# A two-layer decoder in split fp32: the first layer's operand sums, the B sums of its first chunk, the sweep's weights and the modulation's columns are placed anew

## The chip, the core and the metric

The kernel runs on one NeuronCore of a Trainium2 chip. The core has a matrix engine (TensorE, PE in the profile; PEld is its loading of weights), VectorE (DVE), ScalarE (ACT), GpSimd (POOL) and SyncE (SP), which work through queues of their own, each in order, and wait for one another by semaphores. Sixteen DMA engines move data between the chip's memory and the core's. The metric is the device time of one execution in microseconds (us); lower is better. The time before is the median of three runs.

## What is computed

A sequence of 512 tokens of width 1024 goes through two layers; each is a mixer and an MLP, both modulated by a vector `c`:

```python
def modulate(h, shift, scale):
    return h * (1.0 + scale[:, None, :]) + shift[:, None, :]
...
ada = silu(c) @ ada_w + ada_b        # six vectors a layer: shift, scale, gain, twice
h = modulate(rmsnorm(x, g), shift, scale)
x = x + gain * mixer(h)              # layer 0: pooling, layer 1: spatial gating (SGU)
h = modulate(rmsnorm(x, g), shift, scale)
x = x + gain * (square(relu(h @ w1)) @ w2)   # width 1024 -> 4096 -> 1024
```

This is a condensed form of the reference. All of it is float32. In the SGU, `z = gelu(h @ w_in)` is split into u and v, v is normed and mixed along the tokens by `w_s`, and `(u * mixed) @ w_out` is the mixer's output.

## The kernel before

**Products in three parts.** Each float32 operand is split into a high and a low part of the type that TensorE takes. For weights, `split` has ScalarE write `wh` (line 176) and VectorE write `wl` (line 177); for activations `parts` does the same (lines 620 and 621, `oh`/`ol`, `hb`, `as`). `mm3` makes one product of three matmuls: `wl` by high (line 186), `wh` by low (187), `wh` by high (189); in the second product of an MLP the activations are the stationary side and the names stand the other way round. A weight thus passes DMA, ScalarE and VectorE before TensorE can use it, and both engines take such steps strictly in their order.

**The MLP in units.** Both matrix products are cut into blocks and partly done by Strassen and Winograd's scheme of seven products. `mlp` runs a list of `units` in a fixed order on TensorE:

- f(c,f): column tile f of column chunk c of the first product, plain: 48 matmuls of 256 columns.
- s(c,j,m): product m of Strassen's seven for half j of chunk c of the first product: 24 matmuls of 256 columns.
- p(c,m): product m of the seven of the second product over chunk c: 24 matmuls of 512 columns.
- q(dh,t): the last plain part of the second product.

The seven come in the order 1, 5, 6, 3, 7, 2, 4. In layer 0 a sweep of seven column tiles over all of the depth comes first (`sweep_load`, `sweep_hi`, `sweep_lo`; weights `wk`, seven times 128 columns wide), then unit 0 is f(0,7), units 1 to 3 are f(1,0) to f(1,2), and 4 to 15 are p(0,1), f(1,3), p(0,5), f(1,4), p(0,6), f(1,5), p(0,3), f(1,6), p(0,7), f(1,7), p(0,2), p(0,4). Units 16 to 18 are s(2,0,1), s(2,0,5), s(2,0,6), 19 is p(1,1), 20 and 21 are s(2,0,3) and s(2,0,7), 22 is p(1,5); more s and p follow, and 58 to 65 are the q. In layer 1 all column chunks but the first use s units: 0 to 3 are f, 4 to 66 are three rounds of s and p, 67 to 74 the q.

**B sums.** The seven products need sums of w2's blocks. `b_of` loads a block (tile `bt`, one buffer, for the chain; tile `b` otherwise), and `b_add` adds the next block to a tile with an accumulating DMA on GpSimd's queue (line 833). In each chunk `bt` passes m = 1, 5, 6, 4 that way: after each use the next block is added. A fourth accumulating transfer adds block 22 to block 12 for m = 7. The flag `by_dma` is constant here.

**A sums.** In layer 0, `a_parts` (steps at units `A_PARTS`) makes the sums of h's blocks that the s units read (`as`, lines 701, 702, 713, 620, 621). Its scratch is the pool `su`, whose tiles `s` and `u` the p units use too.

**Modulation's columns.** 56 tiles of `ada_w` (tile `ada`, 128x1024, 512 KB each) are loaded by SP's queue (line 205) and reduced by one VectorE operation each (line 209), two of them making a pair of `mods` (line 194). `ex` tells at which unit a tile is issued. In layer 0, `COLUMNS` gives 24 tiles their units; tiles 12 to 18 use the buffer `gb` (one), the others the pool `w4` (three), which the raw weights use too. In the SGU 19 tiles are issued in the u phase, three a step, and five in the output projection (w_o), one a step. In layer 1 eight tiles go to `gb`, at units 8, 10, ... 22. `spread_cols` turns eight `mods` columns into a row by a transpose on TensorE and two DMAs; the row is the MLP's gain.

**What sets the order.** TensorE's order is that of the code. On the other engines a scheduler places each instruction at build time and moves those up that can run, so an operation issued at unit n can stand well ahead of that unit's work. An operation that waits there holds up everything behind it on its engine.

Of the kernel before, what the change touches and what calls it, by code (L numbers as in the profile page):

```python
# [45 lines left out]
def c_g(n, k):  # L46
    return 24 * n + 16 + k
# [29 lines left out]
COLUMNS = (0, 1, 2, 3, 4, 5, 6, 7, 8, 9, 10, 11, 18, 23, 28, 33, 38, 43, 48, 58, 59, 60, 61, 61)  # L77
A_PARTS = (12, 13, 14, 16)
# [3 lines left out]
def decoder_kernel(ctx: ExitStack, tc: tile.TileContext, xtok, vecs, rows, fgrow, ada0, adag, ada1, pool_w, w1s, w1, w1f, w1b, w2, w2e, w_v, w_u, w_o, wsT, lnp, bs, out):  # L82
# [119 lines left out]
    def ada_tile(i, t, src, get):  # L202

        r = get()
        nc.sync.dma_start(r, src)
        b, j = divmod(t, 2)
        if j == 0:
            pmv[i, b] = sm.tile([P, 2], F32, name="pmv", tag="pmv")
        V.scalar_tensor_tensor(r, r, 1.0, cb, ALU.mult, ALU.mult, accum_out=pmv[i, b][:, j : j + 1])  # L209
        if j == 1:  # L210
            finish_mods(i, b, pmv.pop((i, b)))
# [46 lines left out]
    with (  # L258
# [367 lines left out]
    def mlp(i, first, extra, last, ending):  # L626
# [3 lines left out]
        with (  # L630
# [56 lines left out]
            def a_parts(step):  # L687

                blocks = [[H(slice(4 * j, 4 * j + 4), slice(256 * r, 256 * r + 256)) for j in range(2)] for r in range(2)]

                def operand(pool, tag):
                    o = pool.tile([P, 2, 4, 256], F32R, name="as", tag=tag)
                    return o[:, 0], o[:, 1]

                def scratch(tag):
                    return su.tile([P, 4, 256], F32, name="a" + tag, tag=tag)

                def difference(p, q):
                    t, u = scratch("s"), scratch("u")
                    for n, o in enumerate((t, u)):  # L700
                        V.tensor_tensor(o, f32(p[n]), f32(q[n]), ALU.subtract)
                    V.tensor_tensor(t, t, u, ALU.add)
# [120 lines left out]
            by_dma = True  # L823
            held = {}

            def b_of(c, r, n, chain=False):
                kw = dict(name="bt", tag="bt", bufs=1) if by_dma and chain else dict(name="b", tag="b", bufs=3 - by_dma)
# [7 lines left out]
            def p_prep(u):  # L835
# [9 lines left out]
                elif m == 5:  # L845
                    wb = B["t"]
                    if not by_dma:
# [4 lines left out]
                elif m == 6:  # L852
                    wb = B["t"]
                    if not by_dma:
# [6 lines left out]
                elif m == 3:  # L861
                    if by_dma:
                        wb = b_of(c, 1, 1)
                        B["b12"] = b_of(c, 0, 1)
                    else:
                        wb = B["b22"]
                    a = B.pop("s")
                    V.tensor_tensor(a, quad(c, 0, 1), a, ALU.add)
                elif m == 7:
                    wb = B.pop("b12")  # L870
                    if not by_dma:
                        V.tensor_tensor(wb, wb, B.pop("b22"), ALU.add)
                    a = B.pop("u")
                elif m == 2:
                    wb = B["b21"] = b_of(c, 1, 0)
                    a = quad(c, 0, 1)
                else:
                    wb, b21 = B.pop("t"), B.pop("b21")
                    if not by_dma:
                        V.tensor_tensor(wb, wb, b21, ALU.add)  # L880
# [5 lines left out]
                if by_dma:  # L886

                    nxt = {1: 5, 5: 6, 6: 4}.get(m)
                    if nxt:
                        b_add(wb, c, *CHAIN[nxt])  # L890
                    if m == 3:
                        b_add(B["b12"], c, 1, 1)
# [43 lines left out]
            def q_prep(u):  # L936
# [8 lines left out]
                else:  # L945
                    o = w2p.tile([P, 2, KD, P], F32R, name="qo", tag="b", bufs=3 - by_dma)
# [135 lines left out]

    def modulation(q, get):

        return lambda: ada_tile(0 if q < 8 else 1, 40 + q if q < 8 else q - 8, ada1[q], get)
# [17 lines left out]
    with (  # L1103
# [42 lines left out]
        ex += [modulation(q, get4) for q in range(32, 43)]  # L1146
# [33 lines left out]
        ex += [modulation(q, get4) for q in range(43, 48)]  # L1180
        h_[0] = hparts(GAP)
        h32.append(ytile("h32").rearrange("p t d -> p (t d)").rearrange("p (k s) -> p k s", k=KD))
        for dh in range(2):
# [4 lines left out]
            for t, ks in ((0, range(early)), (1, range(early)), (0, range(early, KD)), (1, range(early, KD)), (2, range(KD)), (3, range(KD))):  # L1188
# [57 lines left out]
    ex = [(8 + 2 * q, modulation(48 + q, late_gb if q == 0 else get_gb)) for q in range(8)]  # L1246
    ex += [(30, lambda: spread_cols(mods[1][:, c_g(1, 0) : c_g(1, 0) + KD], "gain1"))]
# [81 lines left out]
```

## Time and profile before

| | us |
|---|---|
| median of 3 runs | 899.78 (895.88 to 901.6) |
| the profiled execution | 898.25 |
| its span in the profile | 896.5 |
| TensorE busy | 857.0 (96%) |
| VectorE busy | 685.5 (76%) |
| ScalarE busy | 467.8 (52%) |
| mean granted clock of TensorE | 0.989 |

The profile is of one execution. A row of the timeline gives start, duration, engine, line and operation, and in brackets how long the engine stood idle before it and what ended that idle time. Matmuls overlap: each is shown some 0.28 or 0.39 us long, while the next starts earlier. The granted clock of TensorE is 1.00 over most of the span and 0.50 in a few spells of 3.4 or 6.8 us. The views by stretch of time give the busy time of each engine within it, so that a stage can be read apart from the mean.

### The profile page before, as it was taken

To read this page: it belongs to the slowest core of one execution; us is meant where nothing else is said; L and a number is where in the kernel's file an instruction comes from. 1 tells how busy PE (TensorE), PEld (TensorE's weight loads), DVE (VectorE), ACT (ScalarE), POOL (GpSimd) and SP (SyncE) were. 2 spreads that over 40 slices of the span, in tenths; PEclk is the share of its full clock that TensorE was granted. 3 is DMA by queue.
4 is the path that set the end of the run, shared out by engine and by line. 5 is a ranking of instruction groups with operands and counts; after the bars stand their busy time and mean duration, and the time that the engine had idled before them with its cause. 6 is when DMAs were issued, how large, how long until landed. Compare 5 with 4: busy or idle time off the path is not lost. (4 is left out here: it accounts for less than half of the span.)

```text
span 896.5 us, 13013 instructions
## 1 busy us (share of the span) xinstructions
PE 857.0 (96%) x5116; PEld 758.1 (85%) x5116; DVE 685.5 (76%) x918; ACT 467.8 (52%) x682; POOL 66.7 (7%) x91
## 2 busy tenths in 40 slices
PE   8999998897999999999999999999897999999996
PEld 7778997786899989888888778999896999989885
DVE  6889466897898688677798856666788698779855
ACT  5285636344576377347332325665755476547521
POOL 3000000001001010000010001000001110110001
PEclk9999999998999999999999999999999999999999
DMA  8968986768587866535748613946787877767402
GB/s 353 417 242 309 347 247 188 227 225 218 125 228 196 202 143 236 212 118 211 245 155 267 210 57 147 323 101 168 190 280 192 204 182 241 165 146 249 145 24 94
DMA packets 43507, 184.43 MB, mean 206 GB/s; under 512 B 4892, under 2 KB 5044, under 8 KB 36151
## 3 DMA queue, kind: packets, MB, share of 16 engines
q1 hardware_dynamic: 35282, 137.72, 41.9%
q0 software_dynamic: 7728, 43.53, 23.9%
q10 hardware_dynamic: 436, 2.37, 0.8%
q8 instruction: 40, 0.66, 0.3%
q14 instruction: 21, 0.16, 0.1%
HBM read 177.29 MB, written 6.30 MB: 205 GB/s over the span
## 5 line engine op out<-in xcount | busy, mean ns | idle before, releaser
L186 PE MATMUL po<-hb,wl 128*128 128x256 f32 (+1 forms) x696 | 207.3, 298 | 3.7 <-DVE wl L177 3.2
L187 PE MATMUL po<-hb,wh 128*128 128x256 f32 (+1 forms) x696 | 206.1, 296 | 0.2 <-DVE hb L621 0.2
L189 PE MATMUL po<-hb,wh 128*128 128x256 f32 (+1 forms) x697 | 205.9, 296 | 0.0
L177 DVE TENSOR_TENSOR wl<-raw,wh 128x1024 fp32r<-128x1024 f32 (+1 forms) x122 | 145.4, 1195 | 32.7 <-ACT wh L176 32.5
L176 ACT ACTIVATE wh<-raw 128x1024 fp32r<-128x1024 f32 (+1 forms) x122 | 125.5, 1034 | 76.9 <-DVE raw L774 22.5
L186 PEld LDWEIGHTS po<-hb,wl 128*128 128x128 f32 x696 | 131.4, 189 | 9.4 <-DVE wl L177 3.1
L187 PE MATMUL pm<-wl,oh 128*128 128x512 f32 x336 | 131.5, 391 | 5.0 <-DVE wl L177 5.0
L187 PEld LDWEIGHTS po<-hb,wh 128*128 128x128 f32 x696 | 132.0, 190 | 4.6 <-DVE hb L621 0.4
L189 PEld LDWEIGHTS po<-hb,wh 128*128 128x128 f32 x697 | 131.9, 189 | 4.3
L186 PE MATMUL pm<-wh,ol 128*128 128x512 f32 x336 | 131.4, 391 | 1.3 <-DVE ol L621 1.2
L189 PE MATMUL pm<-wh,oh 128*128 128x512 f32 (+1 forms) x375 | 131.2, 367 | 0.0
L209 DVE SCALAR_TENSOR_TENSOR ada<-ada,cb 128x1024 f32<-128x1024 f32 x56 | 68.3, 1221 | 53.7 <-DMA ada<-in_ada 53.4
L177 DVE TENSOR_TENSOR wl<-bt,wh 128x1024 fp32r<-128x1024 f32 x48 | 57.8, 1222 | 45.0 <-ACT wh L176 45.0
L189 PEld LDWEIGHTS pm<-wh,oh 128*128 128x128 f32 x375 | 70.5, 188 | 14.8
L186 PE MATMUL po<-as,wl 128*128 128x256 f32 x240 | 69.1, 288 | 13.6 <-ACT g L810 8.2
L176 ACT ACTIVATE wh<-bt 128x1024 fp32r<-128x1024 f32 x48 | 49.5, 1052 | 61.0 <-DMA bt<-in_w 54.7
L187 PEld LDWEIGHTS pm<-wl,oh 128*128 128x128 f32 x336 | 63.2, 188 | 17.7 <-DVE wl L177 6.1
L186 PEld LDWEIGHTS pm<-wh,ol 128*128 128x128 f32 x336 | 63.2, 188 | 13.8 <-DVE ol L621 1.9
L189 PE MATMUL po<-as,wh 128*128 128x256 f32 x240 | 68.3, 285 | 0.0
L187 PE MATMUL po<-as,wh 128*128 128x256 f32 x240 | 68.3, 285 | 0.0
L186 PEld LDWEIGHTS po<-as,wl 128*128 128x128 f32 x240 | 47.0, 196 | 14.9 <-ACT g L810 8.6
L1037 ACT ACTIVATE tmp<-x 128x512 f32<-128x512 f32 (+1 forms) x25 | 15.3, 612 | 66.8 <-DVE x L1033 53.0
(216 smaller groups left out, 1555.4 us busy)
## 6 DMA issues: line engine op xcount, KB each, us to landing
ada<-in_ada SPq DMA_DIRECT2D x72, 512.0 KB, 4.6
raw<-in_w1b SPq DMA_DIRECT2D x40, 512.0 KB, 5.6
b<-in_w SPq DMA_DIRECT2D x18, 1024.0 KB, 5.7
bt<-in_w POOLq DMA_DIRECT2D x18, 1024.0 KB, 8.7
raw<-in_w1b POOLq DMA_DIRECT2D x20, 512.0 KB, 5.6
raw<-in_w2e SPq DMA_DIRECT2D x16, 512.0 KB, 3.6
bt<-in_w SPq DMA_DIRECT2D x6, 1024.0 KB, 8.4
b<-in_w POOLq DMA_DIRECT2D x6, 1024.0 KB, 9.7
```

The lines of the kernel that those rows point to most:

```text
L176: A.activation(h[:, c], r[:, c], AF.Copy)
L177: V.tensor_tensor(l[:, c], r[:, c], f32(h[:, c]), ALU.subtract)
L186: T.matmul(o, wl, mh, start=first, stop=False, **kw)
L187: T.matmul(o, wh, ml, start=False, stop=False, **kw)
L189: T.matmul(o[:, c], wh, mh[:, c], start=False, stop=last and c.stop is None, **kw)
L209: V.scalar_tensor_tensor(r, r, 1.0, cb, ALU.mult, ALU.mult, accum_out=pmv[i, b][:, j : j + 1])
L1037: A.activation(tmp, xt, AF.Square, scale=D**-0.5, accum_out=s[:, len(cs) : len(cs) + 1])
```

## The change

- *A's sums*: `A_PARTS` from (12, 13, 14, 16) to (6, 8, 10, 15); the two scratch tiles of `difference` come from `gb` and `w4` (both tagged `ada`) instead of from `su`.
- *B sums*: in chunk 0 of layer 0 the blocks for m = 5 and m = 6 are loaded as tiles `b` and added on VectorE; the accumulating transfers that did this, two of them, are left out. Block 22 then serves m = 3 too. The rest stays.
- *The sweep's weights*: `wh` and `wl` of the sweep begin `LINE - GAP` words into their tiles instead of at 0.
- *Modulation*: new units for the 24 tiles of layer 0; tiles 8 to 15 are loaded at unit n into `gb`, and their VectorE operation is issued at n + 4 and made to follow a small ScalarE copy out of the latest `wh`. `spread_cols` moves from 53 to 52. The SGU's u phase takes 16 tiles, its output projection eight, two a step. Layer 1's eight are done the late way at 8, 13, ... 43, and its `spread_cols` moves from unit 30 to 48.

```diff
-COLUMNS = (0, 1, 2, 3, 4, 5, 6, 7, 8, 9, 10, 11, 18, 23, 28, 33, 38, 43, 48, 58, 59, 60, 61, 61)
-A_PARTS = (12, 13, 14, 16)
+COLUMNS = (0, 1, 2, 3, 5, 9, 12, 14, 17, 21, 25, 29, 34, 38, 42, 46, 57, 58, 58, 59, 59, 60, 60, 61)
+A_PARTS = (6, 8, 10, 15)
...
+        if late:
+            A.activation(pmv[i, b][:, j : j + 1], f32(latest[0])[:, 0:1], AF.Copy)
         V.scalar_tensor_tensor(r, r, 1.0, cb, ALU.mult, ALU.mult, accum_out=pmv[i, b][:, j : j + 1])
...
-            wk[k] += [t[:, 0 : P * SWEEP] for t in wpair()]
+            wk[k] += [t[:, LINE - GAP : LINE - GAP + P * SWEEP] for t in wpair()]
...
-                    t, u = scratch("s"), scratch("u")
+                    t, u = (r.rearrange("p (k c) -> p k c", k=4) for r in (get_gb(), get4()))
...
-            by_dma = True
+            def by_dma(c):
+
+                return (i, c) != (0, 0)
...
-                    if not by_dma:
+                    if not by_dma(c):
                         B["b12"] = b_of(c, 0, 1)
                         V.tensor_tensor(wb, wb, B["b12"], ALU.add)
...
+                nxt = {1: 5, 5: 6, 6: 4}.get(m)
+                if nxt == 4 or nxt and by_dma(c):
+                    b_add(wb, c, *CHAIN[nxt])
+                if m == 3:
+                    b_add(B["b12"], c, 1, 1)
...
+    def modulation_late(q, n, get):
+
+        r = []
+        return [(n, lambda: r.append(ada_load(ada1[q], get))), (n + 4, lambda: ada_tile(*column_at(q), r[0], True))]
...
-    ex = [(n, modulation(q, get_gb if 12 <= q < 19 else get4)) for q, n in enumerate(COLUMNS)]
-    ex.insert(19, (53, lambda: spread_cols(mods[0][:, c_g(1, 0) : c_g(1, 0) + KD], "gain0")))
+    ex = [(n, modulation(q, get4)) for q, n in enumerate(COLUMNS[:8])]
+    for q in range(8, 16):
+        ex += modulation_late(q, COLUMNS[q], get_gb)
+    ex += [(52, lambda: spread_cols(mods[0][:, c_g(1, 0) : c_g(1, 0) + KD], "gain0"))]
+    ex += [(n, modulation(q, get4)) for q, n in enumerate(COLUMNS) if q >= 16]
...
-        ex += [modulation(q, get4) for q in range(32, 43)]
+        ex += [modulation(q, get4) for q in range(32, 40)]
...
-        ex += [modulation(q, get4) for q in range(43, 48)]
+        ex += [modulation(q, get4) for q in range(40, 48)]
...
-                    if ex:
-                        ex.pop(0)()
+                    for _ in range(2):
+                        if ex:
+                            ex.pop(0)()
...
-    ex = [(8 + 2 * q, modulation(48 + q, late_gb if q == 0 else get_gb)) for q in range(8)]
-    ex += [(30, lambda: spread_cols(mods[1][:, c_g(1, 0) : c_g(1, 0) + KD], "gain1"))]
+    ex = [x for q in range(8) for x in modulation_late(48 + q, 8 + 5 * q, late_gb if q == 0 else get_gb)]
+    ex += [(48, lambda: spread_cols(mods[1][:, c_g(1, 0) : c_g(1, 0) + KD], "gain1"))]
```

How the instructions stand in the built programs, at three places. VectorE in layer 0, from p(0,1) on: `ada,pmv<-ada,cb` is a modulation column, `wl<-bt` and `wl<-raw` the low parts of weights of p and f units, `s` and `ol` the p units' activations. Before:

```order
L209 SCALAR_TENSOR_TENSOR ada,pmv<-ada,cb 128x1024
L177 TENSOR_TENSOR wl<-bt,wh 128x1024
L194 TENSOR_TENSOR mods_89<-pmv,vec 128x2
L209 SCALAR_TENSOR_TENSOR ada,pmv<-ada,cb 128x1024
L177 TENSOR_TENSOR wl<-bt,wh 128x1024
L209 SCALAR_TENSOR_TENSOR ada,pmv<-ada,cb 128x1024
L177 TENSOR_TENSOR wl<-raw,wh 128x1024
L194 TENSOR_TENSOR mods_89<-pmv,vec 128x2
L621 TENSOR_TENSOR ol<-s,oh 128x1024
L209 SCALAR_TENSOR_TENSOR ada,pmv<-ada,cb 128x1024
L177 TENSOR_TENSOR wl<-bt,wh 128x1024
```

Now, where `ada<-hb` and `ada<-ada` are steps of A's sums and `bt<-bt,b` is an addition of B's blocks:

```order
L214 SCALAR_TENSOR_TENSOR ada,pmv<-ada,cb 128x1024
L704 TENSOR_TENSOR ada<-hb 128x1024
L627 TENSOR_TENSOR ol<-s,oh 128x1024
L177 TENSOR_TENSOR wl<-bt,wh 128x1024
L864 TENSOR_TENSOR s<-s,g 128x1024
L705 TENSOR_TENSOR ada<-ada 128x1024
L177 TENSOR_TENSOR wl<-bt,wh 128x1024
L862 TENSOR_TENSOR bt<-bt,b 128x2048
L177 TENSOR_TENSOR wl<-raw,wh 128x1024
L627 TENSOR_TENSOR as<-ada,as 128x1024
L627 TENSOR_TENSOR ol<-s,oh 128x1024
L177 TENSOR_TENSOR wl<-bt,wh 128x1024
```

Of the four columns between the wl of p(0,5), f(1,4) and p(0,6) one is left; A's sums and one addition stand there.

VectorE in the SGU, at the last `gtl` (low part of the gated product, which the output projection reads; `po<-po,wsbs` and `u<-po,u` make it). Before:

```order
L1171 TENSOR_TENSOR u<-po,u 128x512
L198 SCALAR_TENSOR_TENSOR scl_94<-mods_90,vec 128x1
L209 SCALAR_TENSOR_TENSOR ada,pmv<-ada,cb 128x1024
L1175 TENSOR_TENSOR gtl<-u,gth 128x512
L194 TENSOR_TENSOR mods_90<-pmv,vec 128x2
L209 SCALAR_TENSOR_TENSOR ada,pmv<-ada,cb 128x1024
L198 SCALAR_TENSOR_TENSOR scl_94<-mods_90,vec 128x1
L1170 TENSOR_TENSOR po<-po,wsbs 128x512
L177 TENSOR_TENSOR wl<-raw,wh 128x1024
```

Now:

```order
L214 SCALAR_TENSOR_TENSOR ada,pmv<-ada,cb 128x1024
L198 SCALAR_TENSOR_TENSOR scl_94<-mods_90,vec 128x1
L214 SCALAR_TENSOR_TENSOR ada,pmv<-ada,cb 128x1024
L1182 TENSOR_TENSOR po<-po,wsbs 128x512 x2
L1183 TENSOR_TENSOR u<-po,u 128x512 x2
L194 TENSOR_TENSOR mods_90<-pmv,vec 128x2
L1187 TENSOR_TENSOR gtl<-u,gth 128x512
L198 SCALAR_TENSOR_TENSOR scl_94<-mods_90,vec 128x1
L214 SCALAR_TENSOR_TENSOR ada,pmv<-ada,cb 128x1024
L1187 TENSOR_TENSOR gtl<-u,gth 128x512
```

Before, the last column stood ahead of the last two steps of `po<-po,wsbs`; now two stand there together and one more comes between the last two `gtl`.

TensorE, VectorE and ScalarE in layer 1, at the transpose of `spread_cols` (`pb<-ident,mods_90`). TensorE before, ahead of unit 30:

```order
L187 MATMUL po<-as,wh 128x256
L189 MATMUL po<-as,wh 128x256
L236 MATMUL pb<-ident,mods_90 8x128
L186 MATMUL po<-hb,wl 128x256
L187 MATMUL po<-hb,wh 128x256
```

TensorE now, ahead of unit 48, s(3,0,6):

```order
L187 MATMUL po<-as,wh 128x256
L189 MATMUL po<-as,wh 128x256
L241 MATMUL pb<-ident,mods_90 8x128
L186 MATMUL po<-as,wl 128x256
L187 MATMUL po<-as,wh 128x256
```

VectorE now, around the last column and the `mods` that the transpose reads:

```order
L177 TENSOR_TENSOR wl<-raw,wh 128x1024
L214 SCALAR_TENSOR_TENSOR ada,pmv<-ada,cb 128x1024
L177 TENSOR_TENSOR wl<-raw,wh 128x1024
L194 TENSOR_TENSOR mods_90<-pmv,vec 128x2
L864 TENSOR_TENSOR s<-s,g 128x1024
```

The transpose moved by 18 units, and between the last column and its `mods` stands the wl of a later unit. On ScalarE its wh now stands behind the g that copies out s(3,0,5), the unit that ends right before the transpose:

```order
L813 ACTIVATE g<-po 128x2x256
L176 ACTIVATE wh<-raw 128x1024
L213 ACTIVATE pmv<-wh 128x1
L813 ACTIVATE g<-po 128x2x256
L176 ACTIVATE wh<-raw 128x1024
L243 ACTIVATE line<-pb 8x128
```

More of the change, by code (lines that the diff above doesn't have):

```diff
@@ L200, in decoder_kernel, with ada_load, ada_tile @@
     pmv = {}
-    def ada_tile(i, t, src, get):
+    def ada_load(src, get):
         r = get()
         nc.sync.dma_start(r, src)
+        return r
+    def ada_tile(i, t, r, late=False):
         b, j = divmod(t, 2)
@@ L819, in s_run @@
                 square(t)
-            by_dma = True
             held = {}
+            def by_dma(c):
+                return (i, c) != (0, 0)
             def b_of(c, r, n, chain=False):
-                kw = dict(name="bt", tag="bt", bufs=1) if by_dma and chain else dict(name="b", tag="b", bufs=3 - by_dma)
+                kw = dict(name="bt", tag="bt", bufs=1) if chain else dict(name="b", tag="b", bufs=2)
                 t = w2p.tile([P, 4, S], F32, **kw)
@@ L853, in p_prep @@
                     wb = B["t"]
-                    if not by_dma:
+                    if not by_dma(c):
                         B["b22"] = b_of(c, 1, 1)
@@ L861, in p_prep @@
                 elif m == 3:
-                    if by_dma:
+                    if by_dma(c):
                         wb = b_of(c, 1, 1)
@@ L870, in p_prep @@
                     wb = B.pop("b12")
[L871 to L872 removed]
                     a = B.pop("u")
                 elif m == 2:
[L875 removed]
+                    wb = b_of(c, 1, 0)
                     a = quad(c, 0, 1)
                 else:
[L878 to L880 removed]
+                    wb = B.pop("t")
                     a = quad(c, 1, 1)
@@ L1081, in first0, with column_at @@
         return SWEEP
+    def column_at(q):
+        return (0, 40 + q) if q < 8 else (1, q - 8)
     def modulation(q, get):
-        return lambda: ada_tile(0 if q < 8 else 1, 40 + q if q < 8 else q - 8, ada1[q], get)
+        return lambda: ada_tile(*column_at(q), ada_load(ada1[q], get))
+    def modulation_late(q, n, get):
+        r = []
+        return [(n, lambda: r.append(ada_load(ada1[q], get))), (n + 4, lambda: ada_tile(*column_at(q), r[0], True))]
     def ending0():
```

12 lines of the change are left out of this document (2 added, 10 removed).

## The prediction

> **What bounds the kernel now.** I read the page first, then TensorE's waits by stretch of time, then the timelines of the engines that end those waits. Row of the page, and rows of the windows view (start:end, length, then busy us of PE, PEld, DVE, ACT and POOL, the granted clock, DMA share, GB/s):
>
> ```profile
> PE 857.0 (96%) x5116; PEld 758.1 (85%) x5116; DVE 685.5 (76%) x918; ACT 467.8 (52%) x682; POOL 66.7 (7%) x91
> ...
> 120.00:240.00 120.00, 105.22 (x653) 94.24 (x652) 91.02 (x108) 55.28 (x71) 6.01 (x7) 0.96 0.72 206
> 240.00:300.00 60.00, 60.00 (x392) 54.52 (x391) 52.24 (x56) 37.55 (x46) 6.05 (x7) 1.00 0.79 200
> 300.00:420.00 120.00, 119.74 (x682) 104.83 (x681) 93.09 (x125) 68.00 (x96) 9.57 (x13) 1.00 0.57 181
> ...
> 500.00:520.00 20.00, 17.53 (x79) 13.76 (x78) 15.36 (x27) 5.50 (x8) 0.00 (x0) 0.94 0.54 180
> 640.00:700.00 60.00, 52.13 (x341) 47.60 (x339) 50.00 (x56) 35.47 (x46) 4.86 (x6) 0.97 0.81 223
> ```
>
> TensorE is the bound, and of its 39.5 us of idle time (896.5 - 857.0) 14.8 lie in 120 to 240, 7.9 in 640 to 700 and 2.5 in 500 to 520: the three places that the change touches. From 240 to 300 it never waits, beside a VectorE that is 87% busy. TensorE's timeline (start, duration, and in brackets idle time and releaser) gives the first place its price:
>
> ```profile
> 122.62 0.39 PE L186 MATMUL pm<-wh,ol 128*128 128x512 f32 x1
> ...
> 128.06 0.29 PE L186 MATMUL po<-hb,wl 128*128 128x256 f32 x1
> ...
> 141.46 0.38 PE L186 MATMUL po<-hb,wl 128*128 128x256 f32 x1 [2.05 <-DVE wl L177]
> ...
> 168.05 0.50 PE L187 MATMUL pm<-wl,oh 128*128 128x512 f32 x1 [3.36 <-DVE wl L177]
> ...
> 234.98 0.29 PE L186 MATMUL po<-hb,wl 128*128 128x256 f32 x1
> ```
>
> p(0,1) starts at 122.62 and the unit behind it at 128.06: an undisturbed p or f unit takes 5.44. Units 4 to 22 of layer 0 are fourteen such and five s units of half the matmuls (2.72): 14 x 5.44 + 5 x 2.72 = 89.8 us. They took 234.98 - 122.62 = 112.4. So 22.6 us are lost there: 14.8 as idle time, about 4.7 as matmuls at half clock (windows below: 3.40 busy us and 6.01 at 0.50), the rest as the pipeline's refills.
>
> Why TensorE waits there is in VectorE's groups from 120 to 184 and in the timelines of VectorE and ScalarE:
>
> ```profile
> L209 DVE SCALAR_TENSOR_TENSOR ada<-ada,cb 128x1024 f32<-128x1024 f32 x11 | 13.5, 1223 | 21.2 <-DMA ada<-in_ada 21.2
> ...
> 131.46 1.23 DVE L209 SCALAR_TENSOR_TENSOR ada<-ada,cb 128x1024 f32<-128x1024 f32 x1 [8.29 <-DMA ada<-in_ada]
> ...
> 133.75 0.15 DVE L194 TENSOR_TENSOR mods<-pmv,vec 128x2 f32<-128x2 f32 x1
> ...
> 139.03 1.23 DVE L209 SCALAR_TENSOR_TENSOR ada<-ada,cb 128x1024 f32<-128x1024 f32 x1 [2.85 <-DMA ada<-in_ada]
> 140.19 0.08 DVE L209 DVE_READ_ACCUMULATOR ada<-ada,cb 128x1 f32 x1
> 140.19 1.22 DVE L177 TENSOR_TENSOR wl<-raw,wh 128x1024 fp32r<-128x1024 f32 x1
> ...
> 130.74 1.06 ACT L176 ACTIVATE wh<-bt 128x1024 fp32r<-128x1024 f32 x1 [10.62 <-DMA bt<-in_w]
> ...
> 145.38 1.06 ACT L176 ACTIVATE wh<-bt 128x1024 fp32r<-128x1024 f32 x1 [8.25 <-DMA bt<-in_w]
> ...
> 175.65 1.06 ACT L620 ACTIVATE as<-as 128x1024 fp32r<-128x1024 f32 x1 [11.82 <-DVE as L702]
> ```
>
> VectorE stood still 21.2 us for modulation columns, with weights' wl behind them in its queue: the wl at 140.19 follows the column of 139.03 and releases the matmul at 141.46. ScalarE stood 10.62 and 8.25 for accumulated B sums, then 11.82 for A's sums.
>
> **The change part by part.** *Columns in layer 0.* From 120 to 184 stood 11 modulation operations; over the same units four remain (the order), each behind ScalarE's copy of a later wh. Seven times 1.22 leave VectorE, and 3.5 MB leave the queues. *B sums.* Two accumulating transfers go. Two adds of 128x2048 come; no such row exists, and the nearest is two operations of 128x1024:
>
> ```profile
> 630.66 2.35 DVE L177 TENSOR_TENSOR wl<-bt,wh 128x1024 fp32r<-128x1024 f32 x2
> ```
>
> so 2 x 2.35 = 4.7 us (bounds 0 and twice that), less than the 8.5 us of the seven operations gone. *A's sums* come one to six units sooner in other buffers: the same operations, and the 11.82 us should go. Walking the new order with these durations, VectorE stays 2 to 6 us ahead of TensorE through chunk 0. What stays late is chunk 1's accumulation, unchanged by the edit; in before it was issued and landed (POOL's row, then ScalarE's) thus:
>
> ```profile
> 213.00 0.87 POOL L833 DMA_DIRECT2D bt<-in_w  x1 [1.42 <-DVE wl L177]
> ...
> 223.52 2.01 ACT L176 ACTIVATE wh<-bt 128x1024 fp32r<-128x1024 f32 x2 [6.01 <-DMA bt<-in_w]
> ```
>
> 10.5 us. From its issue in the new order I get 1.2 to 2.7 us of wait at the s unit 21 and 1 to 2 more at p(1,5): 3.8 us in all. Gain of the stage: 22.6 - 3.8 = 18.8 (bounds: 22.6 with nothing left, 0 with every wait back elsewhere). Six of the operations taken out come back in chunks 1 and 2; the 7.8 idle us of VectorE in 240 to 300 alone nearly cover 6 x 1.31 = 7.9. I charge 1 us (bounds 0 and 7.9).
>
> *Layer 1.* Rows of TensorE, VectorE and ScalarE:
>
> ```profile
> 645.06 0.36 PE L186 MATMUL po<-as,wl 128*128 128x256 f32 x1 [2.84 <-DVE wl L177]
> ...
> 694.61 0.38 PE L186 MATMUL po<-as,wl 128*128 128x256 f32 x1 [4.51 <-ACT g L810]
> ...
> 642.54 1.23 DVE L209 SCALAR_TENSOR_TENSOR ada<-ada,cb 128x1024 f32<-128x1024 f32 x1 [3.50 <-DMA ada<-in_ada]
> 643.70 0.08 DVE L209 DVE_READ_ACCUMULATOR ada<-ada,cb 128x1 f32 x1
> 643.70 1.22 DVE L177 TENSOR_TENSOR wl<-raw,wh 128x1024 fp32r<-128x1024 f32 x1
> ...
> 693.96 0.59 ACT L810 ACTIVATE g<-po 128x512 f32<-128x512 f32 x1
> 694.44 1.07 ACT L176 ACTIVATE wh<-raw 128x1024 fp32r<-128x1024 f32 x1
> ```
>
> The column of 642.54 costs 2.84 on TensorE. The 4.51 at 694.61 ends a VectorE backlog, in which three operations fewer will now stand. With 1.6 at reduced clock (4 us at 0.59, below), 9 us are there to gain; I take 8.5. A new wait comes: the transpose that spreads the gains moves to unit 48 and needs the last mods, which on VectorE stand behind a wl, whose wh on ScalarE stands behind the g that reads the s unit just finished. TensorE idles from that unit's end: the last matmul's own 0.29, g 0.59, wh 1.07, wl 1.22, mods 0.15 = 3.32, taken as 3.4 for the steps between engines. Net 5.1 (bounds: 9 if the wait is hidden, -5 if nothing is gained and the clock falls as well).
>
> *The clock after a wait*, by the windows view:
>
> ```profile
> 142.30:145.70 3.40, 3.40 (x19) 3.40 (x18) 0.31 (x1) 0.32 (x1) 0.00 (x0) 0.50 0.99 331
> ...
> 168.05:175.00 6.95, 6.95 (x50) 6.53 (x51) 6.81 (x11) 0.00 (x0) 0.00 (x0) 1.00 0.92 348
> 210.60:217.40 6.80, 6.01 (x26) 5.92 (x27) 6.80 (x7) 4.66 (x7) 1.72 (x2) 0.50 0.98 210
> ...
> 694.60:698.60 4.00, 3.99 (x21) 3.99 (x22) 3.97 (x4) 2.33 (x3) 0.85 (x1) 0.59 1.03 189
> ```
>
> A 2.05 us wait (141.46) was followed by 3.4 us at 0.50; one of 3.36 (168.05) by none. So the new wait costs 3.4 by the one and 3.4 + 1.7 = 5.1 by the other; I take the row nearest in length, 3.4. The Trainium skill (TensorE: Matmul & The Clock Gate, "What's actually happening") says the clock is halved after at least one idle window of about 3.4 us, and restored after as long a busy one. By that rule a 3.4 us wait sits on the edge, and the sum would be 1.7 us worse. The trace agrees on the 3.4 us of half clock but not on the idle time needed, 2.05 us having been enough once.
>
> *The SGU's output projection.* Rows of TensorE, VectorE, SP's queue and the page's list of DMA issues (last column: us to landing):
>
> ```profile
> 517.72 0.76 PE L186 MATMUL po<-wh,gtl 128*128 128x512 f32 x1 [1.03 <-DVE gtl L1175]
> ...
> 501.01 1.23 DVE L209 SCALAR_TENSOR_TENSOR ada<-ada,cb 128x1024 f32<-128x1024 f32 x1 [1.55 <-DMA ada<-in_ada]
> ...
> 496.60 8.42 SPq L205 DMA_DIRECT2D ada<-in_ada  x4
> ...
> ada<-in_ada SPq DMA_DIRECT2D x72, 512.0 KB, 4.6
> ```
>
> Four columns stood ahead of the last gtl; the order now has eight, and on SP's queue eight loads ahead of w_o's second half. Their loads chain through w4's buffers. With 4.6 + 1.23 each for those that share a buffer I find both last gtl within 1 us of where they were: 0 (bounds: +4, and the four added wholly unhidden, 4 x 5.83 = -23.3).
>
> *Sweep.* Group of the sweep's first matmul (min/median/max ns) and, from the page, a group of the same shape elsewhere:
>
> ```profile
> L589 PE MATMUL po<-hb,wl x16: 392/398/504, 60.6 to 95.6; 128*128 128x512 f32 x16
> ...
> L187 PE MATMUL pm<-wl,oh 128*128 128x512 f32 x336 | 131.5, 391 | 5.0 <-DVE wl L177 5.0
> ```
>
> 7 ns longer, on 8 x 7 x 3 = 168 matmuls: 1.2 us to gain if the place in the line is the cause (bounds 0 and 2).
>
> Sum: 18.8 - 1 + 5.1 + 0 + 1.2 = 24.1. The profiled execution took 898.25 us, 1.75 of it outside its span; 898.25 - 24.1 = 874.2. The median of three runs, 899.78, lies 1.5 above that execution: 875.7, so 876.
>
> **The rivals.** *Chunk 1's accumulations take over.* Each of its three chained transfers takes about 10 us, and TensorE now arrives some 18 us sooner. If each costs 3 to 4 us more, half of the stage's gain goes: 876 + 9.4 = 885.4. For it: the 6.01 at 223.52. Against it: the whole chain starts sooner too, and the 2 MB and 3.5 MB less in the queues before it.
>
> *VectorE becomes the bound in chunks 1 and 2.* It is busy 52.24 of 60 us in a stretch without waits; if the six operations added there find no gap, they go straight to TensorE: 7.9, less the 1 charged: 876 + 6.9 = 883. Against it: from 300 to 420 it is idle for 120 - 93.09 = 26.9 us, and columns are read by nothing until their layer's next stage, so that they may fall behind.
>
> *Slower: the w_o stage starves.* The eight loads come in one line; if they land not in 4.6 but in 10.5 us, as the accumulated load of 213.00 did, each added column costs 10.5 + 1.23 and four of them 46.9, and w_o's second half waits behind them: 876 + 46.9 = 923. It decides from 24/4 - 1.23 = 4.8 us of unhidden landing time on each: hardly above the page's 4.6, but only if nothing of it is hidden. Against it: before, 8.42 us for four issues at 496.60 cost TensorE 2.5 in all.
>
> *Only the columns matter.* If A's sums and B's adds change nothing, what remains is the 21.2 us of VectorE's waits, of which about half, 10.6, would have reached TensorE: 876 + 18.8 - 10.6 = 884.
>
> **How the numbers follow.** Forecast 0.60, with a range of its own from 868 to 882; chunk 1's accumulations 0.14; VectorE as bound 0.12; only the columns 0.06; the w_o stage 0.04; and 0.04 for more than one wait gone that I kept, under 868. The clock rule is inside the forecast's range (878). The range reaches over the rivals at 883 to 885 with some spread, 867 to 889. About 1% is what a measurement of this kernel can tell from no change: faster means under 890.8. The forecast, the gains beyond it and nearly all of the three cases from 883 to 885 do that: 0.88; same 0.08; slower 0.04.
>
> **What would show it.** Right: in the new profile no idle VectorE for columns between units 4 and 15, TensorE at 19.5 or more of each 20 us there, one bracket of some 3.4 us in front of the transpose in layer 1, none at f(1,4). Wrong: brackets of bt at units 19 to 24, VectorE at 100% with TensorE waiting for wl in chunk 1 or 2, waits for gtl or w_o's wl over 5 us, or columns still waited for.

## The result and the profile after

| | before | after |
|---|---|---|
| median of 4 runs, us | 897.83 (895.66 to 901.6) | 874.6 (871.8 to 874.96) |
| span of the profiled execution, us | 896.5 | 872.9 |
| TensorE busy, us | 857.0 | 846.1 |
| VectorE busy, us | 685.5 | 689.4 |

The ratio is 0.973, with a 95% interval from 0.9686 to 0.9774. TensorE waits now for these (the waits view of the changed kernel: engine and line, what it waited for, us in total, times, longest):

```profile
PE pb L241 <- DVE mods L194: 5.6, 1, 5.6
PE po L186 <- DVE wl L177: 3.7, 3, 1.8
PE pg L419 <- DMA ada<-in_adag: 2.5, 2, 1.5
PE px L1061 <- ACT xs L1054: 2.3, 1, 2.3
```

The longest wait is new: it is the one of the transpose in layer 1. The windows of the changed kernel (busy us of PE, PEld, DVE, ACT, POOL, then clock, DMA share, GB/s):

```profile
118.00:206.00 88.00, 87.52 (x584) 79.97 (x583) 76.33 (x77) 52.20 (x66) 6.23 (x7) 1.00 0.67 184
205.00:300.00 95.00, 92.72 (x611) 84.28 (x611) 78.60 (x93) 54.37 (x72) 8.26 (x10) 1.00 0.78 214
...
480.00:505.00 25.00, 23.56 (x115) 19.32 (x114) 23.32 (x44) 6.83 (x11) 0.00 (x0) 1.00 0.65 217
610.00:670.00 60.00, 60.00 (x403) 54.97 (x402) 52.67 (x56) 41.70 (x57) 5.98 (x7) 1.00 0.83 217
743.00:755.00 12.00, 7.82 (x35) 7.40 (x36) 5.88 (x8) 2.43 (x4) 1.64 (x3) 0.72 0.77 194
```

From 118 to 206 TensorE is idle for half a microsecond, and the clock stays at 1.00. The stage that was priced in the prediction, from the first matmul of p(0,1) to the first behind p(1,5), now reads on TensorE's timeline:

```profile
120.68 0.40 PE L186 MATMUL pm<-wh,ol 128*128 128x512 f32 x1
...
211.53 0.29 PE L186 MATMUL po<-hb,wl 128*128 128x256 f32 x1
...
227.26 0.36 PE L186 MATMUL po<-as,wl 128*128 128x256 f32 x1 [1.72 <-DVE wl L177]
...
306.69 0.36 PE L186 MATMUL po<-as,wl 128*128 128x256 f32 x1 [1.79 <-DVE wl L177]
...
385.96 0.33 PE L1061 MATMUL px<-ident,xs 128*128 128x128 f32 x1 [2.35 <-ACT xs L1054]
```

It takes 90.8 us in place of 112.4, one more than its matmuls need without a wait (89.8). VectorE's groups over the same units, now:

```profile
L214 DVE SCALAR_TENSOR_TENSOR ada<-ada,cb 128x1024 f32<-128x1024 f32 x4 | 4.9, 1222 | 4.8 <-DMA ada<-in_ada 4.8
...
L862 DVE TENSOR_TENSOR bt<-bt,b 128x2048 f32<-128x2048 f32 x1 | 2.3, 2292 | 0.0
L855 DVE TENSOR_TENSOR bt<-bt,b 128x2048 f32<-128x2048 f32 x1 | 2.3, 2285 | 0.0
```

Four columns, with 4.8 us of waiting that no matmul sees, and the two additions at 2.29 us each.

Both programs have the same matmuls in almost the same order, so their profiles can be laid side by side by counting matmuls. Between the same ones, in us:

| stretch | before | after | gain |
|---|---|---|---|
| head, up to the sweep | 59.5 | 58.6 | 0.9 |
| sweep | 37.8 | 36.8 | 1.0 |
| p(0,1) to p(1,5) | 112.4 | 90.8 | 21.5 |
| rest of chunks 1 and 2, layer 0 | 129.1 | 133.6 | -4.5 |
| norm and SGU up to w_o | 98.1 | 100.8 | -2.7 |
| w_o and the next norm's start | 40.1 | 37.1 | 2.9 |
| layer 1, first units | 71.9 | 69.9 | 2.1 |
| layer 1, first round and some more | 88.0 | 77.4 | 10.6 |
| around the transpose | 12.1 | 20.7 | -8.5 |

The gains are rounded from the unrounded lengths. What is left out of the table changed by 0.6 us or less; with it the gains make up the 23.6 us between the spans.

### The profile page after: what moved, and what is told of

The parts are those of the page before. It is cut to its first block, busy times and chain, and to the rows that moved or that the text cites. A ratio compares the mean times of both kernels' runs of the same rounds, so it can differ in the third digit from the quotient of the medians.

```text
span 872.9 us, 13040 instructions
## 1 busy us (share of the span) xinstructions
PE 846.1 (97%) x5116; PEld 751.5 (86%) x5116; DVE 689.4 (79%) x920; ACT 469.0 (54%) x698; POOL 65.1 (7%) x89
## 3 DMA queue, kind: packets, MB, share of 16 engines
q0 software_dynamic: 7440, 41.43, 23.2%
## 4 chain that ended last, share of the span: by engine, by line
PE 70%; DMA 11%; DVE 11%; ACT 4%; issue 2%; POOL 1%; SPq 0%; POOLq 0%; DVEq 0%; ACTq 0%
PE po L186 13%; PE po L187 13%; PE po L189 13%; PE pm L187 10%; PE pm L189 10%; PE pm L186 10%; DMA ada<-in_ada 4%; DVE wl L177 4%; DMA wh<-in_ada 2%; DMA bt<-in_w 2%; DVE ada L214 2%; ACT wh L176 2%; DMA wl<-in_ada 1%; DMA ada<-in_adag 1%; DVE v L1153 1%
## 5 line engine op out<-in xcount | busy, mean ns | idle before, releaser
L186 PE MATMUL po<-hb,wl 128*128 128x256 f32 (+1 forms) x696 | 205.2, 295 | 0.2 <-DVE wl L177 0.2
L177 DVE TENSOR_TENSOR wl<-raw,wh 128x1024 fp32r<-128x1024 f32 (+1 forms) x122 | 145.8, 1200 | 35.9 <-ACT wh L176 35.9
L176 ACT ACTIVATE wh<-raw 128x1024 fp32r<-128x1024 f32 (+1 forms) x122 | 125.5, 1035 | 90.4 <-DVE raw L777 30.7
L177 DVE TENSOR_TENSOR wl<-b,wh 128x1024 fp32r<-128x1024 f32 x36 | 43.3, 1221 | 7.5 <-ACT wh L176 7.5
```

The costliest lines, as they stand in the source:

```text
L176: A.activation(h[:, c], r[:, c], AF.Copy)
L177: V.tensor_tensor(l[:, c], r[:, c], f32(h[:, c]), ALU.subtract)
L186: T.matmul(o, wl, mh, start=first, stop=False, **kw)
```

## The experiments

Each kernel was compared with the kernel before on the same chip. "Stage" is the stretch from p(0,1) to p(1,5), "rest" that of chunks 1 and 2 behind it, both between the same matmuls as above.

| run | median us | ratio, 95% interval | stage | rest |
|---|---|---|---|---|
| the change | 874.6 | 0.973 (0.9686 to 0.9774) | 90.8 | 133.6 |
| spread at 56 | 867.28 | 0.967 (0.965 to 0.9691) | 90.4 | 132.7 |
| late columns every 4 units | 868.52 | 0.9681 (0.966 to 0.9703) | 90.6 | 134.1 |
| columns alone | 889.58 | 0.9923 (0.9899 to 0.9947) | 102.3 | 131.5 |
| both sums alone | 888.69 | 0.9903 (0.9879 to 0.9927) | 98.0 | 138.3 |
| B sums alone | 890.56 | 0.9895 (0.9858 to 0.9932) | 109.2 | 129.3 |
| columns and B sums | 879.11 | 0.979 (0.974 to 0.984) | 90.1 | 132.9 |
| the change, B sums by DMA | 885.64 | 0.988 (0.9838 to 0.9923) | 103.3 | 133.7 |
| the change, A's sums late | 870.38 | 0.9719 (0.9685 to 0.9753) | 90.1 | 132.8 |

**The transpose.** Two kernels, each with one edit to the changed one. The first:

```diff
-    ex += [(48, lambda: spread_cols(mods[1][:, c_g(1, 0) : c_g(1, 0) + KD], "gain1"))]
+    ex += [(56, lambda: spread_cols(mods[1][:, c_g(1, 0) : c_g(1, 0) + KD], "gain1"))]
```

> The changed kernel with layer 1's spread of the gains at unit 56 instead of 48. Theory: the transpose's wait of 5.62 us at 747.18 is there only because the transpose stands on TensorE before the mods it reads; the spell at half clock behind it (6.8 us, so 3.4 lost) is its consequence. Both go: 874.6 - 9.0 = about 866 us, no wait in front of the transpose. Rival: VectorE is late there as a whole, and the next units wait in its place: 872 to 875, with new waits for wl or ol between 745 and 755.

The second leaves the transpose and moves the columns:

```diff
-    ex = [x for q in range(8) for x in modulation_late(48 + q, 8 + 5 * q, late_gb if q == 0 else get_gb)]
+    ex = [x for q in range(8) for x in modulation_late(48 + q, 8 + 4 * q, late_gb if q == 0 else get_gb)]
```

> The changed kernel with layer 1's late columns issued every 4 units (8, 12, ... 36) instead of every 5; the transpose stays at 48. Theory: the last mods are done some 5 units sooner, the wait in front of the transpose goes: about 866 us. Rival: the denser columns bring back waits for wl in the first round of layer 1 (up to 3 us) or the last column is late all the same: 870 to 875.

867.28 and 868.52 us, some 1 and 2.5 us over what the theories had. The windows view of the first, over the time in which the changed kernel was busy for 7.82 us at a clock of 0.72:

```profile
743.00:755.00 12.00, 12.00 (x85) 11.09 (x84) 7.88 (x11) 6.30 (x7) 0.86 (x1) 1.00 0.68 176
```

The wait was the transpose's: in its place there is only one of 0.81 us, at 741.27, for a g of ScalarE, and the half clock went too. Either end of the wait can be moved. Why it was 5.62 us long shows on VectorE's timeline of the changed kernel:

```profile
740.05 2.35 DVE L177 TENSOR_TENSOR wl<-bt,wh 128x1024 fp32r<-128x1024 f32 x2
742.33 1.22 DVE L627 TENSOR_TENSOR ol<-s,oh 128x1024 fp32r<-128x1024 f32 x1
743.46 1.22 DVE L177 TENSOR_TENSOR wl<-raw,wh 128x1024 fp32r<-128x1024 f32 x1
744.60 1.22 DVE L214 SCALAR_TENSOR_TENSOR ada<-ada,cb 128x1024 f32<-128x1024 f32 x1
745.74 0.09 DVE L214 DVE_READ_ACCUMULATOR ada<-ada,cb 128x1 f32 x1
745.74 1.22 DVE L177 TENSOR_TENSOR wl<-raw,wh 128x1024 fp32r<-128x1024 f32 x1
746.88 0.16 DVE L194 TENSOR_TENSOR mods<-pmv,vec 128x2 f32<-128x2 f32 x1
```

and on ScalarE's:

```profile
742.10 0.58 ACT L813 ACTIVATE g<-po 128x512 f32<-128x512 f32 x1
742.58 1.05 ACT L176 ACTIVATE wh<-raw 128x1024 fp32r<-128x1024 f32 x1
```

TensorE's last matmul ahead of the transpose starts at 741.28. ScalarE is done with the wh at 743.63, as the prediction's chain had it; but VectorE works without a pause from 740.05, has three operations of the p unit and a wl ahead of the column, and comes to the wl behind the column only at 745.74.

**The first stage, part by part.** The columns of layer 0 alone, put into the kernel before:

```diff
-COLUMNS = (0, 1, 2, 3, 4, 5, 6, 7, 8, 9, 10, 11, 18, 23, 28, 33, 38, 43, 48, 58, 59, 60, 61, 61)
+COLUMNS = (0, 1, 2, 3, 5, 9, 12, 14, 17, 21, 25, 29, 34, 38, 42, 46, 57, 58, 58, 59, 59, 60, 60, 61)
...
+    for q in range(8, 16):
+        ex += modulation_late(q, COLUMNS[q], get_gb)
...
```

> The kernel before with only layer 0's columns of the change (units, late way, spread at 52). The stage from p(0,1) to p(1,5) took 112.4 us before and 91.2 after. Theory (all three edits are needed): VectorE's waits for columns (21.2 us from 120 to 184) go, but A's sums stay late and the B chain stays on GpSimd's queue: about half of the 21 us, 886 to 888 us; ScalarE still waits some 8 us for bt in chunk 0. Rival (only the columns matter): 21 us in this stage, 877 to 880 us. Second rival (columns were only waiting where something else was late): under 4 us gain, over 893.

The sums alone, put into the kernel before:

```diff
-A_PARTS = (12, 13, 14, 16)
+A_PARTS = (6, 8, 10, 15)
...
-                    t, u = scratch("s"), scratch("u")
+                    t, u = (r.rearrange("p (k c) -> p k c", k=4) for r in (get_gb(), get4()))
...
+                return (i, c) != (0, 0)
...
```

> The kernel before with only the sums of the change: A's sums at units 6, 8, 10, 15 with scratch in gb and w4, and chunk 0's first two B sums on VectorE. Columns as before. Theory (all needed): about 5 to 9 us gain, 889 to 893 us; VectorE still waits over 10 us for columns between 120 and 184. Rival (only the columns matter): 896 or more. Second rival (the sums are what mattered): 878 to 881.

889.58 and 888.69: each brings some 8 us, about as expected. Of the columns' part, 4.9 us lie in w_o and in layer 1's first units, which that edit does not touch. In the stage the columns bring 10.1 and the sums 14.4; the sums give 9.2 back in chunks 1 and 2, where seven of the old columns now stand and two did before. With the columns alone the accumulated sums remain late (ScalarE's timeline of that run):

```profile
129.56 1.06 ACT L176 ACTIVATE wh<-bt 128x1024 fp32r<-128x1024 f32 x1 [9.67 <-DMA bt<-in_w]
...
142.75 1.06 ACT L176 ACTIVATE wh<-bt 128x1024 fp32r<-128x1024 f32 x1 [6.78 <-DMA bt<-in_w]
```

One thing came otherwise than expected: VectorE's waits for columns did not go. From 118 to 182 four columns still wait 15.5 us (VectorE's groups of that run), where eleven waited 21.2 before:

```profile
L214 DVE SCALAR_TENSOR_TENSOR ada<-ada,cb 128x1024 f32<-128x1024 f32 x4 | 4.9, 1221 | 15.5 <-DMA ada<-in_ada 15.5
```

Half of it is one column whose load landed 11.65 us after its issue (SP's queue and VectorE's timeline of that run):

```profile
117.20 0.33 SPq L204 DMA_DIRECT2D ada<-in_ada  x1
...
128.85 1.23 DVE L214 SCALAR_TENSOR_TENSOR ada<-ada,cb 128x1024 f32<-128x1024 f32 x1 [8.18 <-DMA ada<-in_ada]
```

In the changed kernel the same load had landed within 4.43 us of its issue, and its column did not wait:

```profile
116.55 0.33 SPq L204 DMA_DIRECT2D ada<-in_ada  x1
...
120.98 1.22 DVE L214 SCALAR_TENSOR_TENSOR ada<-ada,cb 128x1024 f32<-128x1024 f32 x1
```

With the columns alone, GpSimd had issued two accumulating transfers shortly before that load, at 113.97 and 116.35; in the changed kernel it issues the first at 119.44, behind it. By these rows the accumulating transfers land late themselves, and a column's load that runs beside them does too.

Next, in the changed kernel, the two sums undone one at a time. B sums:

```diff
             def by_dma(c):
-                return (i, c) != (0, 0)
+                return True
```

> The changed kernel with chunk 0's B sums left to accumulating DMAs, as before; A's sums and the columns stay changed. The stage from p(0,1) to p(1,5) takes 90.8 us in the changed kernel and 102.3 with the columns alone, so both sums together are worth 11.5 there. Theory: the two accumulations each hold ScalarE's wh of bt by 8 us and more, and some 4 to 8 us of it reach TensorE: 879 to 883 us. Rival (with the columns gone the transfers land in time): 873 to 876.

A's sums:

```diff
-A_PARTS = (6, 8, 10, 15)
+A_PARTS = (12, 13, 14, 16)
...
-                    t, u = (r.rearrange("p (k c) -> p k c", k=4) for r in (get_gb(), get4()))
+                    t, u = scratch("s"), scratch("u")
```

> The changed kernel with A's sums as before: at units 12, 13, 14 and 16, scratch in the tiles that the p units use. Theory: VectorE has the room, but the s units 16 to 21 find their operands late and waits of 4 to 8 us come back in front of s(2,0,3) and s(2,0,7): 879 to 883 us; with the run that undoes the B sums the losses add up to about 11 us. Rival (the B sums are worth all of it): 873 to 876.

This went otherwise than expected. Without the B sums the stage takes 103.3 us, 12.5 more, which is all that the two sums were worth behind the columns; the median, 885.64, lies above even the theory's 883. The column loaded at 117.16 waits again, until 129.67, and VectorE's four columns wait 20.5 us in all. Without the early A's sums the stage takes 90.1, no more than with them: there the rival holds, the B sums being worth all of it, and 870.38 us is less than its 873. TensorE's timeline of the run with B by DMA:

```profile
134.37 0.76 PE L187 MATMUL pm<-wl,oh 128*128 128x512 f32 x1 [1.85 <-DVE wl L177]
...
140.25 0.50 PE L187 MATMUL pm<-wl,oh 128*128 128x512 f32 x1 [1.29 <-DVE wl L177]
...
150.29 0.50 PE L186 MATMUL pm<-wh,ol 128*128 128x512 f32 x1 [1.78 <-ACT wh L176]
...
152.22 0.79 PE L187 MATMUL pm<-wl,oh 128*128 128x512 f32 x1 [1.43 <-DVE wl L177]
```

and ScalarE's, with its waits for the accumulated tile:

```profile
130.91 1.06 ACT L176 ACTIVATE wh<-bt 128x1024 fp32r<-128x1024 f32 x1 [11.05 <-DMA bt<-in_w]
...
149.18 1.06 ACT L176 ACTIVATE wh<-bt 128x1024 fp32r<-128x1024 f32 x1 [4.84 <-DMA bt<-in_w]
```

So the question was whether B's sums do this without the columns' move too. B sums alone in the kernel before (`by_dma(c)` as in the change, nothing else):

> The kernel before with only chunk 0's first two B sums on VectorE. Theory, as the last runs leave it: in the stage from p(0,1) to p(1,5) what counts is the columns' waits on VectorE and the accumulations' waits on ScalarE, and A's sums count for nothing. With both sums changed the stage took 98.0 us. Then this run's stage takes 98 to 101 us too, the time is 887 to 891. Rival (A's sums made that part of the gain while the old columns stood there): stage 106 or more, time 893 or more.

And the columns with the B sums, nothing else of the change:

> The kernel before with layer 0's columns and chunk 0's B sums of the change, and nothing else of it. Theory: the stage takes 90 to 91 us as in the whole change; with 4.5 us lost in chunks 1 and 2 and 2.7 at the next norm, and layer 1 as before: 896.5 - 21.5 + 4 + 2.5 - 4 = 877 to 880 us, 19 us from two edits that alone brought 8 and (expected) 8. Rival (the two simply add): 881 to 883.

B alone: 109.2 us in the stage, a gain of 3.2. By the stage the rival holds: with the old columns in place A's sums did matter, since both sums took the stage to 98.0. The time, 890.56, is the one that the theory named, for another reason (below). ScalarE's groups of that run, from 118 to 220, name what is late then:

```profile
L176 ACT ACTIVATE wh<-bt 128x1024 fp32r<-128x1024 f32 x10 | 10.3, 1053 | 13.6 <-DMA bt<-in_w 7.1 <-DVE bt L859 6.4
...
L620 ACT ACTIVATE as<-as 128x1024 fp32r<-128x1024 f32 x3 | 3.2, 1062 | 24.1 <-DVE as L702 12.6 <-DVE as L713 11.4
```

The additions themselves wait in VectorE's queue (6.4), and ScalarE waits for A's sums as long as before (24.1 us; 23.2 in the kernel before). Its median is 8.8 us under the one before, more than its stage shows; in the profiles 4.8 us of that lie in w_o and in layer 1's first units, which it does not touch, of which more below. Columns with B: 90.1 us in the stage and 879.11 in all, as the theory had it. Two edits that bring 10.1 and 3.2 us of the stage alone bring 22.3 together. VectorE's waits for columns from 118 to 184 go the same way: 15.5 us with the columns alone, 10.0 with B alone, 5.6 with both.

To see whether early A's sums cost something elsewhere, the run with A's sums late having the lower median, they were put back beside the spread at 56:

> The changed kernel with the spread at unit 56 and A's sums as before (units 12, 13, 14, 16; scratch in the p units' tiles). Theory: once the columns are out of chunk 0 the time of A's sums is worth nothing either way: 866 to 868 us, a ratio of 0.967 as with the spread alone. Rival (sooner sums cost some 4 us, as the median of the run with A's sums late could be read): 862 to 864.

866.86 us (ratio 0.9639, 0.9611 to 0.9666), against 867.28 with them early: no difference that can be told.

**The losses behind the stage.** Two edits on top of the spread at 56. Layer 0's last eight columns sooner:

```diff
-... 42, 46, 57, 58, 58, 59, 59, 60, 60, 61)
+... 42, 46, 50, 51, 53, 54, 55, 56, 57, 58)
```

> The kernel with the spread at unit 56, and layer 0's last eight columns at units 50 to 58 instead of 57 to 61. In the changed kernel TensorE waits 2.35 us at 385.96 for xs of the next norm, 2.7 us over the whole of that stage against before. Theory: two columns stand on VectorE ahead of the residual sums that xs needs; sooner, they free it and 2 us are gained: 865. Rival: the columns wait for their loads in front of wl or of the last p units and cost as much or more there: 867 to 872.

869.36 us. The norm's wait is gone and that stretch takes 98.2 us, as it did before the change (98.1), but the q units ahead of it take 41.8 in place of 37.9, and the rest of chunks 1 and 2 135.1: the rival holds. Chunk 1's sums on VectorE too:

```diff
-                return (i, c) != (0, 0)
+                return (i, c) not in ((0, 0), (0, 1))
```

> The kernel with the spread at unit 56, and chunk 1's B sums on VectorE too. The changed kernel waits 1.72 us at 227.26 and 0.56 at 271.85 behind a bt that landed late (ScalarE idle 5.07 us for it). Theory (the chain on GpSimd's queue is what bounds chunk 1): those waits go, 865 to 866. Rival (VectorE, 83% busy there, becomes the bound with 4.7 us more): new waits for wl, 868 to 872.

867.38 us, the same as without it. The waits at 227 and 272 went (the one at 306, behind chunk 2's sums, stayed), and a new one stands in the chunk (TensorE's timeline, then VectorE's load in the windows view of this run):

```profile
218.12 0.50 PE L186 MATMUL pm<-wh,ol 128*128 128x512 f32 x1 [1.17 <-DVE ol L627]
```

```profile
205.00:300.00 95.00, 93.20 (x610) 84.27 (x609) 81.53 (x94) 56.93 (x74) 7.74 (x9) 1.00 0.75 209
```

Neither theory's price came: the work went from the queue of transfers to VectorE, now 86% busy, and brought as much as it cost.

**The sweep.** In the changed kernel, its weights at word 0 of their tiles again:

```diff
-            wk[k] += [t[:, LINE - GAP : LINE - GAP + P * SWEEP] for t in wpair()]
+            wk[k] += [t[:, 0 : P * SWEEP] for t in wpair()]
```

> The changed kernel with the sweep's weights at word 0 of their tiles again. Theory (the place in the tile's line is the cause): the sweep's matmuls come 233 ns apart instead of 227, the stretch from the sweep's start to f(0,7) takes 37.8 us instead of 36.8. Rival (the pitch is a state that depends on something else): 36.8.

37.8 us, as the theory had it. Of all the profiles, the six of kernels with the weights at word 0 show 37.8 there and the eight with the new place 36.8. One execution took 873.34; a microsecond is not to be told from that, the place in the profile is.

## Why the prediction was right

The forecast was 876 and the measured median 874.6. Its sum of 24.1 us stands against 23.6 us between the spans, but that is partly luck: several terms were off, in both directions. The terms to which it gave a size came to 20.1 us (21.5 - 4.5 + 10.6 - 8.5 + 1.0); the other 3.5 came from w_o, which it put at 0 (2.9), and from places that it left out: layer 1's first units (2.1), the head (0.9) and the norm (-2.7). Its own signs were not all met: VectorE still waits 4.8 us for columns, and ScalarE waits 4.64 and 5.07 us for late bt (199.84 and 214.91), though only the second shows on TensorE, behind the stage.

*The stage in layer 0: 18.8 forecast, 21.5 measured.* The place and the mechanism were right, the size was short, because the 3.8 us that the prediction kept for chunk 1's accumulation at s unit 21 and p(1,5) did not come there. The account of the parts was wrong in one step: "the 11.82 us should go", as a gain of the A's sums, is no separate gain. That wait of ScalarE was a consequence of the other two: it is 9.42 us with the columns alone and 0.39 with the columns and the B sums, A's sums being late in both, and late sums cost nothing then (stage 90.1). The two causes are the columns and the accumulations, and each hides much of the other; the accumulations also held up a column's load, which the prediction did not see. Whether it is the smaller number of columns or their tie to a later wh that counts, no run separates. The rival that only the columns matter is out, as the columns alone leave the stage at 102.3; its own estimate of their part, 10.6 us, is near the 10.1 measured.

*Chunks 1 and 2: -1 forecast, -4.5 measured.* This term was mis-sized, because it was priced by VectorE's room for six more operations. VectorE has as much idle time in that stretch as before (20.8 us; 21.4 before), and no column there waits for its load. What came is waits of TensorE behind accumulated sums that land late, 4.1 us in all against 0.3 before. ScalarE's timeline of the changed kernel:

```profile
214.91 1.07 ACT L176 ACTIVATE wh<-bt 128x1024 fp32r<-128x1024 f32 x1 [5.07 <-DMA bt<-in_w]
...
223.60 0.64 ACT L821 ACTIVATE g<-g 128x512 f32<-128x512 f32 x1 [3.60 <-DVE g L816]
...
294.27 1.06 ACT L176 ACTIVATE wh<-bt 128x1024 fp32r<-128x1024 f32 x1 [3.71 <-DMA bt<-in_w]
```

and VectorE's:

```profile
225.89 1.23 DVE L177 TENSOR_TENSOR wl<-raw,wh 128x1024 fp32r<-128x1024 f32 x1 [1.19 <-ACT wh L176]
```

Behind the late bt VectorE pauses once, for 1.19 us, ahead of the wl for which the matmul at 227.26 waits, and this pause is for a wh of ScalarE's, which had itself waited 3.60 us for VectorE. No column stands in between. So waits of the size that the prediction put at s unit 21 and p(1,5), 3.8 us, came later, outside the stage, one of them in chunk 2: the two terms together were forecast at 17.8 and gave 17.0. How much the columns themselves cost there, no run shows (with the columns alone the stretch takes 131.5 us, 2.4 more than before). The rival on the accumulations thus named the cause, but asked about twice what came (9.4 us); taking chunk 1's chain away alone moved the wait to VectorE and left the time, so the rival on VectorE as the bound stood right behind it.

*Layer 1's waits: 8.5 forecast, 10.6 measured*, all of the waits and the slow clock of that stretch, and some more. In every profile that keeps the old columns of layer 1 this stretch takes 88.0 to 89.7 us, in every one with the new 77.3 to 78.0. Which of the edits there does it (the later units, the tie to a later wh, the transpose's move away from unit 30) no run separates.

*The transpose: 3.4 forecast, 8.5 measured.* The wait was foreseen in its place and its cause; its size failed in the step "g 0.59, wh 1.07, wl 1.22, mods 0.15", which follows ScalarE's queue and takes VectorE to be free when the wh is ready. It was not, and the wait became 5.62. Such a wait brought the clock down, which the prediction had weighed for one of 3.4 us and left out, though in the profile before a wait of 3.70 us (211.39) already went with 6.8 us at 0.50. The windows view of the changed kernel shows the spell:

```profile
746.18:753.00 6.82, 5.82 (x27) 5.75 (x28) 1.99 (x3) 0.56 (x2) 0.55 (x1) 0.50 0.91 264
```

6.82 us at 0.50, 1.0 of it still idle: some 2.9 us lost. The Trainium skill, as cited in the prediction (TensorE: Matmul & The Clock Gate, "What's actually happening"), has the clock halved after at least one idle window of about 3.4 us. The wait of 5.62 us was longer than that, and the clock was halved; the two lengths of the slow spells, 3.4 and 6.8 us, are about one and two such windows.

*w_o: 0 forecast.* The two last gtl cost TensorE 1.4 us now and 2.2 before, so the change as such moved little, as forecast; the slower rival, with eight loads unhidden, did not come. TensorE's timeline now:

```profile
498.38 0.50 PE L186 MATMUL po<-wh,gtl 128*128 128x512 f32 x1 [0.60 <-DVE gtl L1187]
...
500.19 0.50 PE L186 MATMUL po<-wh,gtl 128*128 128x512 f32 x1 [0.84 <-DVE gtl L1187]
```

The stretch gained 2.9 us all the same, in good part because the spell at half clock of the execution before (517.8 to 521.2) did not recur: the four other kernels that keep the SGU's old columns have 37.3 to 38.8 us there, against 40.1 before, and the nine with the new ones 35.9 to 37.1. So about 1 us of the gain can be the edit's.

*The next norm: not in the sum, -2.7.* The prediction had no term for the columns at units 57 to 61. They come in a row on VectorE ahead of the residual sums, and the first transposes of the norm wait 2.35 us for xs; with the last eight sooner that wait is gone.

*The sweep: 1.2 forecast, 1.0 measured*, by the cause given.

The kernel with the spread at unit 56 is faster than the changed one, 867.28 us; with A's sums late as well it is 866.86, which is not a difference.

## What to carry to other kernels

Two waits in series in front of the same matmuls hide each other: undoing each in the new kernel, and doing each alone in the old, tells what one of them would have been worth, and here an edit that looked like a third cause was worth nothing once the other two were gone. A transfer taken out can also free another that ran beside it, so look at the landing times of both. When a step is moved so that TensorE's order meets a value made late, price it by the whole queue ahead of that value on each engine, not by its chain of dependences alone, and add the spell of slow clock that such a wait can bring. Where nothing needs the result soon, put the consumer later: eight units here gave 7 us.

## What the hardware showed that was not expected

Matmuls of 128x256 with the same operands' places ran at two paces at full clock. In layer 1's first units the kernel before has them 118 ns apart from 571.04 on, behind a break of 0.24 us:

```profile
571.04 0.38 PE L187 MATMUL po<-hb,wh 128*128 128x256 f32 x1 [0.24 <-DVE hb L621]
```

and keeps that pace for some 340 matmuls, to the first p unit; the changed kernel, without that break, has them 113 ns apart. It is worth 2.1 us in the table above. Of the other kernels some show the one pace there and some the other (69.7 to 70.2 us, or 71.6 to 71.7), without regard to which edits they hold: B sums alone has the fast one, columns with B sums the slow one, and the changed kernel with the sweep's weights at 0 the slow one. The break is not its cause: four kernels are at 118 ns from 36 matmuls earlier on, without a break at this matmul, and in the change with B sums by DMA the pace goes from 118 to 113 behind a break there. What sets the pace stays open. It explains, with the spell of half clock, why single profiles differ by 2 to 5 us in stretches that an edit does not touch; since one execution of each kernel was profiled, it is not known how often either recurs.

The length of a wait did not settle what the clock did. The norm's wait of 2.35 us at 385.96 left it at 1.00 in the changed kernel; in the kernel with the spread at 56 the same wait, at 385.07, went with a spell at half clock (its windows view):

```profile
385.04:388.45 3.41, 3.38 (x16) 3.38 (x17) 2.44 (x4) 2.72 (x6) 0.00 (x0) 0.50 0.00 0
```

In front of the transpose a wait of 5.62 us went with 6.8 us at 0.50, one of 5.39 (the sweep's weights at 0) with 3.4.
